# New prices in the clock that orders a hybrid decoder step: weight products, tile changes, scaled copies and a port shared by VectorE and GpSimd

## The chip, the cores and the metric

The kernel runs on one core of one Trainium2 chip. The metric is device time in microseconds (us); a verdict compares medians of several runs. A core has five engines that work at the same time, each through its own list of instructions in order: TensorE (PE, matmuls; PEld is its weight load), VectorE (DVE), ScalarE (ACT), GpSimd (POOL) and SyncE (SP, which issues most transfers). An instruction waits for semaphores of other engines, and everything behind it on its engine waits with it.

## The reference, cut to what matters

One step of a one-layer decoder for a prompt of 256 tokens and eight samples of eight tokens, 320 rows in all, with shared weights:

```python
h = rmsnorm(x, norm_g)
u = h @ w_in                            # 2048 x 23664: inputs of both mixers, gates
o_a = gdn(u) * silu(z_a)                # gated DeltaNet, 16 qk heads, 32 v heads, chunks of 64
o_b = nsa(u) * silu(z_b)                # compressed, selected and window attention over paged caches
y = x + (sigmoid(m_a) * (o_a @ w_branch_a) + sigmoid(m_b) * (o_b @ w_branch_b)) @ w_out
```

The DeltaNet recurrence goes over the chunks of the prompt, for each head:

```python
v_new = u_c - w_c @ s
o = qg_c @ s + attn_c @ v_new
s = s * gl_c + kdec_c.T @ v_new
```

where `u_c` and `w_c` are solutions of a triangular system per chunk. For the samples the state of each (`state_gdn`) is read, stepped by eight tokens and written. In the attention, each sample gathers 16 blocks of keys through a page table.

## The kernel before, in words

**Weight products.** The 320 rows stand on the free axis, the features on the partitions. Weights are read in pieces of up to 1 MB (`wraw`) and split in two parts of a format that TensorE reads faster: ScalarE writes `whi`, a rounded copy, and VectorE or GpSimd `wlo` = `wraw` − `whi`. The rows are split alike (`hhi`, `hlo`; for the branch products `oah`, `oal`). Three products, `hhi`·`whi`, `hlo`·`whi` and `hhi`·`wlo`, each 128x128 by 128x320, add up in `acc`; there are two such accumulators, and 11,952 such products in all. `wpool` holds three pieces, `wsplit` four parts of each kind.

**Stages.** While the weights go by, the other work runs between the products: the norm of the rows, the prompt's attention, the samples' attention over compressed, window and selected pages (two streams of samples with ten page buffers each), then sixteen blocks of the DeltaNet, each for one qk head and its two v heads, and at last the branch products and `w_out`. A DeltaNet block `j` has a convolution (`xp`, `cv`), norms (`sq`, `bank`), the preparation (`kk`, `kq`, `A`, `at`, `R`), the inverse of the triangular system by doubling (`Xd`, `Ac`, `T`, `TTd`, `X`: products of 32x32 tiles with a step of VectorE between them), the chunk steps of the prompt (`vnz` on VectorE, from it on TensorE `p` and `ps`, and the new state `st` on VectorE) and the steps of the samples (`sS`, `vS`, `pu`, `ats`).

**What sets the order.** The order is made while the program is built. Every part is a stream, a Python generator that says before each step which engine it needs and which tiles. `Run.go` takes at each point the stream whose step could start earliest, by a clock that counts along; its rank breaks ties. The product stream `p_mm` has the last rank, 9: a weight product goes out where nothing else could start as early. The streams that split weights (`p_hi`, `p_lo`) come early when the parts run low. `p_lo` gives a part to GpSimd for the first four and, during the DeltaNet, for every fourth; else to VectorE.

The clock (class `Clock`) holds a time for each engine, the end of the last write and read of each tile, and a delay between engines (`WAIT`). `Timed` wraps every engine: it prices an instruction by its kind and size, calls `Clock.op`, which moves the engine's time, and then records the instruction itself. So a price decides where later instructions stand, and nothing else; each engine then runs its list in that order, and the waits between engines follow from the tiles. All recorded instructions have the line of the call in this wrapper (L320 before, L331 after), transfers L292 and L299.

The function `page` issues the read of one cache page. The page's number must be in a register of SyncE; `page` loads the 16 numbers of a sample in one go (`ptab`) when they are not at hand, and drops the numbers of another selected sample of the same parity, or of any compressed one, when it does.

Of the kernel before, what the change touches and what calls it, by code (L numbers as in the profile page):

```python
# [64 lines left out]
class Pack:  # L65
    def __init__(self, rows=P):
        self.at, self.parts, self.n, self.rows = {}, [], 0, rows
# [95 lines left out]
def _n(ap):  # L163
    n = 1
    for x in ap.ap[1:]:
        n *= x[1]
    return n


class Clock:  # L170
# [6 lines left out]
    def __init__(self):  # L177
        self.t = dict.fromkeys(("pe", "act", "dve", "pool", "sp", "dge", "dma"), 0.0)
        self.parts, self.cut, self.psum = {}, {}, set()
        self.slot = {}  # L180
        self.w, self.r = {}, {}
        self.last = (0.0, "sp")
        self.set, self.lock, self.narrow, self.cold = None, False, False, True

    def key(self, ap):
        n = ap.tensor.name
        k = self.slot.get(n)
        if k is None:
            return None
        if k[0] == "dscr":  # L190
            k = k, ap.offset
        if n in self.cut:
            k = k, ap.offset % 512 >= self.cut[n]
        if n in self.parts:
            width, step = self.parts[n]
            row, col = divmod(ap.offset, width)
            k = k, col // P, row // step
        return k
# [43 lines left out]
            self.set = name  # L242
            self.t["act"] += 1300

    def op(self, eng, ns, outs, ins):
        outs, ins = self.keys(outs), self.keys(ins)
        self.t[eng] = e = self.start(eng, outs, ins) + ns
        self.mark(eng, e, outs, ins)

    def dma(self, eng, nbytes, out, in_):  # L250
# [13 lines left out]
def _isap(x):  # L264
    return isinstance(x, bass.AP)


class Timed:


    def __init__(self, eng, name, clock):
        self.__dict__.update(eng=eng, name=name, clock=clock)

    def __getattr__(self, op):
        f = getattr(self.eng, op)
        if op == "preload_act_table_set":
            def f_(name):
                self.clock.table("exp" if name == EXPSET else "sqrt")
                f(name)
            return f_  # L280
        if not callable(f) or op == "value_load":
            return f

        def g(*a, **k):
            aps = [x for x in a if _isap(x)] + [x for n, x in k.items() if _isap(x) and n not in ("out", "accum_out")]
            outs = [x for x in (k.get("out"), k.get("accum_out")) if _isap(x)]
            if "out" not in k:
                outs.insert(0, aps.pop(0))
            n = _n(outs[0])
            if op == "dma_start":  # L290
                self.clock.dma(self.name, 4 * n * outs[0].ap[0][1], outs[0], aps[0])
                return f(*a, **k)  # L292
            if self.name == "pe":
                if op == "transpose":
                    ns = 109
                else:
                    kk, m = a[1].ap[0][1], _n(a[1])
                    if a[1].dtype == F32R:
                        ns = max(n / 2.4, 107)  # L299
                    else:  # L300
                        ns = max(n * 1.67, 107) if m > 32 else max(n / 2.1 + 13, 34)
                narrow = op != "transpose" and _n(a[1]) <= 32
                if self.clock.narrow and not narrow:
                    ns += 80
                self.clock.narrow = narrow
                if self.clock.cold:
                    ns *= 2
            elif self.name == "dve":
                if op in ("tensor_reduce", "reciprocal"):
                    n = _n(a[1])  # L310
                ns = 65 + n * (6.4 if op == "reciprocal" else 1) / 0.96
                if op == "scalar_tensor_tensor" or (op == "tensor_scalar" and len(aps) > 1):
                    ns += 62
            elif self.name == "act":
                self.clock.table(SETS.get(a[2] if len(a) > 2 else k["func"], None))
                ns = (50 if aps[0].tensor.name in self.clock.psum else 93) + n / 1.2 + (170 if "accum_out" in k else 0)
            else:
                ns = 100 + n * (1.9 if op == "tensor_tensor" else 1)
            self.clock.op(self.name, ns, outs, aps)
            return f(*a, **k)  # L320
        return g

# [103 lines left out]
def step(ctx: ExitStack, tc: tile.TileContext, I, O):  # L426
# [854 lines left out]
    def scores(e, b, npg, dst, kS, finish):  # L1281
# [39 lines left out]
        V.scalar_tensor_tensor(dst[:, npg * P:npg * P + 64], ns[:, :64], SCALE, newB[:, 56 - 8 * b:120 - 8 * b], op0=OP.mult, op1=OP.add)  # L1321

    def weighted(e, b, npg, x, vS, op):
        prev = None
        for quad in list(range(0, npg + 1, 4)) + [None]:
# [1003 lines left out]
```

## Time and profile before

| what | value |
| --- | --- |
| median of 3 runs | 2679.83 us (2678.03 to 2683.69) |
| the profiled execution | 2674.97 us, of which the span is 2673.2 |
| TensorE busy | 2578.5 us (96%) |
| VectorE busy | 1714.6 us (64%) |
| ScalarE busy | 1360.4 us (51%) |
| GpSimd busy | 678.1 us (25%) |
| read and written | 543.84 MB, mean 203 GB/s |

The page of the profile counts matmuls as pipelined, so a busy time of TensorE may hold slack. The clock of TensorE that the chip granted had a mean of 0.993. A row of a group reads: line, engine, operation, output <- inputs, tile, count | busy us, mean ns of one | idle us just before them and what ended it.

### The profile page before, as it was taken

To read this page: it belongs to the slowest core of one execution; us is meant where nothing else is said; L and a number is where in the kernel's file an instruction comes from. 1 tells how busy PE (TensorE), PEld (TensorE's weight loads), DVE (VectorE), ACT (ScalarE), POOL (GpSimd) and SP (SyncE) were. 2 spreads that over 40 slices of the span, in tenths; PEclk is the share of its full clock that TensorE was granted. 3 is DMA by queue.
4 is the path that set the end of the run, shared out by engine and by line. 5 is a ranking of instruction groups with operands and counts; after the bars stand their busy time and mean duration, and the time that the engine had idled before them with its cause. 6 is when DMAs were issued, how large, how long until landed. Compare 5 with 4: busy or idle time off the path is not lost. (4 is left out here: it accounts for less than half of the span.)

```text
span 2673.2 us, 58873 instructions
## 1 busy us (share of the span) xinstructions
PE 2578.5 (96%) x22228; PEld 2327.9 (87%) x22228; DVE 1714.6 (64%) x3740; ACT 1360.4 (51%) x3098; POOL 678.1 (25%) x929
## 2 busy tenths in 40 slices
PE   7999999999999999999999899988999989999999
PEld 6898888888888888899889888888988889999999
DVE  5554446555555655445987888988888875355543
ACT  5453443343443333336667666666666655444443
POOL 2000011000000000012454454555445444211111
PEclk9999999999999999999999999999999989999999
DMA  6647676878768898865355445444455456656554
GB/s 205 229 156 257 231 241 228 279 248 282 269 222 308 287 333 283 284 211 175 118 157 175 132 153 176 141 139 136 153 153 166 155 160 214 207 177 192 179 192 132
DMA packets 548671, 543.84 MB, mean 203 GB/s; under 512 B 32482, under 2 KB 452499, under 8 KB 548003
## 3 DMA queue, kind: packets, MB, share of 16 engines
q1 hardware_dynamic: 534308, 493.67, 57.7%
q0 software_dynamic: 14080, 46.41, 4.9%
q8 instruction: 175, 2.87, 0.4%
q14 instruction: 108, 0.88, 0.1%
HBM read 470.31 MB, written 69.67 MB: 202 GB/s over the span
## 5 line engine op out<-in xcount | busy, mean ns | idle before, releaser
L320 PE MATMUL acc<-hhi,whi 128*128 128x320 f32 (+1 forms) x3472 | 1156.1, 333 | 0.8 <-ACT whi L320 0.8
L320 PE MATMUL acc<-hhi,wlo 128*128 128x320 f32 (+1 forms) x3472 | 1078.1, 311 | 2.0 <-DVE wlo L320 1.4
L320 PE MATMUL acc<-hlo,whi 128*128 128x320 f32 (+1 forms) x3472 | 1076.4, 310 | 1.3 <-DVE hlo L320 1.1
L320 ACT ACTIVATE whi<-wraw 128x512 fp32r<-128x512 f32 (+1 forms) x996 | 626.1, 630 | 861.3 <-PE acc L320 791.5
L320 DVE TENSOR_TENSOR wlo<-wraw,whi 128x512 fp32r<-128x512 f32 x838 | 605.0, 725 | 510.0 <-ACT whi L320 503.9
L320 PEld LDWEIGHTS acc<-hhi,whi 128*128 128x128 f32 (+1 forms) x3472 | 657.4, 189 | 80.4 <-issue 65.8
L320 PEld LDWEIGHTS acc<-hlo,whi 128*128 128x128 f32 (+1 forms) x3472 | 657.8, 189 | 8.7 <-issue 2.5
L320 PEld LDWEIGHTS acc<-hhi,wlo 128*128 128x128 f32 (+1 forms) x3472 | 655.6, 189 | 3.6 <-DVE wlo L320 2.6
L320 POOL TENSOR_TENSOR wlo<-wraw,whi 128x512 fp32r<-128x512 f32 (+1 forms) x158 | 208.0, 1317 | 417.9 <-ACT whi L320 391.3
L320 DVE SCALAR_TENSOR_TENSOR cv<-xp,cw,cv 128x344 f32<-128x344 f32 x192 | 141.5, 737 | 28.5 <-ACT cv L320 26.1
L292 POOL DMA_DIRECT2D d_mz<-raw x48 | 26.4, 550 | 519.9 <-ACT raw L320 487.1
L320 PE MATMUL acc<-oah,whi 128*128 128x320 f32 x512 | 158.2, 309 | 0.0
L320 PE MATMUL acc<-oal,whi 128*128 128x320 f32 x512 | 158.2, 309 | 0.0
L320 PE MATMUL acc<-oah,wlo 128*128 128x320 f32 x512 | 158.2, 309 | 0.0
L320 ACT ACTIVATE kT<-nt 128x512 f32<-128x512 f32 x80 | 47.7, 596 | 101.7 <-PE ns L320 55.9
L320 DVE COPY kT<-nt 128x512 f32<-128x512 f32 x80 | 55.2, 691 | 64.5 <-PE ns L320 41.5
L320 PEld LDWEIGHTS acc<-oah,whi 128*128 128x128 f32 x512 | 96.1, 188 | 0.0
L320 PEld LDWEIGHTS acc<-oal,whi 128*128 128x128 f32 x512 | 96.1, 188 | 0.0
L320 PEld LDWEIGHTS acc<-oah,wlo 128*128 128x128 f32 x512 | 96.1, 188 | 0.0
L320 POOL TENSOR_TENSOR vx<-v,pk_gdn 128x512 fp32r<-128x512 f32 x64 | 71.2, 1112 | 74.4 <-DVE v L320 56.1
L320 PE MATMUL pp<-cpg,Pk 128*32 128x512 f32 x608 | 83.0, 602 | 0.0
L320 PE MATMUL nt<-pk_const,spg 128*128 128x128 f32 x512 | 68.3, 274 | 0.5 <-DMA spg<-cache_k_sel 0.5
(420 smaller groups left out, 3629.5 us busy)
## 6 DMA issues: line engine op xcount, KB each, us to landing
wraw<-w_in SPq DMA_DIRECT2D x136, 1024.0 KB
wraw<-w_in SPq DMA_DIRECT2D x97, 512.0 KB
cpg<-cache_k_cmp SPq DMA_DIRECT2D x128, 256.0 KB
cpg<-cache_v_cmp SPq DMA_DIRECT2D x128, 256.0 KB
spg<-cache_k_sel SPq DMA_DIRECT2D x128, 256.0 KB
spg<-cache_v_sel SPq DMA_DIRECT2D x128, 256.0 KB
wraw<-w_branch_a SPq DMA_DIRECT2D x32, 1024.0 KB
sS<-state_gdn SPq DMA_DIRECT2D x32, 512.0 KB
```

The lines of the kernel that those rows point to most:

```text
L292: return f(*a, **k)
L320: return f(*a, **k)
```

## The change

Five prices of the clock change:

1. A product of the fast format (`F32R`): the time for n columns was n / 2.4 ns, at least 107; now (n + 32) / 2.4. For 320 columns 133 and 147 ns.
2. A product in full precision whose stationary tile has at most 32 columns (`m`): was n / 2.1 + 13 ns, at least 34; now n × 0.42, 0.105 or 0.47, at least 13, by the number of rows of that tile (`kk`) and by n.
3. A change of tile size: was 80 ns when TensorE leaves a tile with `m` up to 32; now 170 ns whenever it goes from a full tile to one with 64 or fewer rows or columns, or back.
4. ScalarE: 100 ns more where a copy has a second operand in memory (a scale or bias).
5. A shared port: an operation of VectorE with two inputs in SBUF and a two-input operation of GpSimd cannot overlap; the later one starts at the earlier one's end. The delay goes into the engine's time.

```diff
-    def op(self, eng, ns, outs, ins):
+    def op(self, eng, ns, outs, ins, port=False):
         outs, ins = self.keys(outs), self.keys(ins)
-        self.t[eng] = e = self.start(eng, outs, ins) + ns
+        s = self.start(eng, outs, ins)
+        if port:
+            a, b = self.port["pool" if eng == "dve" else "dve"]
+            if a <= s < b:
+                s = b
+            self.port[eng] = s, s + ns
+        self.t[eng] = e = s + ns
         self.mark(eng, e, outs, ins)
...
                     if a[1].dtype == F32R:
-                        ns = max(n / 2.4, 107)
+                        ns = max((n + 32) / 2.4, 107)
+                    elif m > 32:
+                        ns = max(n * 1.67, 107)
                     else:
-                        ns = max(n * 1.67, 107) if m > 32 else max(n / 2.1 + 13, 34)
-                narrow = op != "transpose" and _n(a[1]) <= 32
-                if self.clock.narrow and not narrow:
-                    ns += 80
-                self.clock.narrow = narrow
+                        ns = max(n * (0.42 if kk > 32 else 0.105 if n > 32 else 0.47), 13)
+                part = op != "transpose" and (kk <= 64 or m <= 64)
+                if self.clock.narrow != part:
+                    ns += 170
+                self.clock.narrow = part
...
+                port = op in ("tensor_tensor", "scalar_tensor_tensor") and sum(x.tensor.name not in self.clock.psum and _n(x) > 1 for x in aps) > 1
...
-                ns = (50 if aps[0].tensor.name in self.clock.psum else 93) + n / 1.2 + (170 if "accum_out" in k else 0)
+                ns = (50 if aps[0].tensor.name in self.clock.psum else 93) + n / 1.2 + (170 if "accum_out" in k else 100 if len(aps) > 1 else 0)
             else:
-                ns = 100 + n * (1.9 if op == "tensor_tensor" else 1)
-            self.clock.op(self.name, ns, outs, aps)
+                port = op == "tensor_tensor"
+                ns = 100 + n * (1.9 if port else 1)
+            self.clock.op(self.name, ns, outs, aps, self.name in ("dve", "pool") and port)
```

The instructions are the same, except for the loads of page numbers; the order differs. Three places follow.

TensorE around the 6576th weight product, in the DeltaNet stage. `p` and `ps` from `vnz` are the chunk steps of the prompt, `st`,`wq` the next one's first product, `kk` and `pu` belong to other blocks and to the samples' steps. Before, a chunk step there:

```order
L320 MATMUL bank<-pk_const,tl 108x128
L320 MATMUL p_20718<-vnz_14558,kde 128x128 x2
L320 MATMUL acc<-hhi,whi 128x320
L320 MATMUL acc<-hlo,whi 128x320
L320 MATMUL acc<-hhi,wlo 128x320
L320 MATMUL ps<-vnz_14558,at 128x128 x2
...
L320 MATMUL ps<-st,wq 128x128 x2
L320 MATMUL bank<-pk_const,hist 128x96
```

Three to six weight products stand between the steps of the recurrence. Now:

```order
L331 MATMUL ps<-R,pk_gdn 128x294
L331 MATMUL p_20981<-vnz_14461,kde 128x128 x2
L331 MATMUL ps<-vnz_14461,at 128x128 x2
L331 MATMUL ps<-st,wq 128x128 x2
L331 MATMUL kk<-kqP 128x128 x2
L331 MATMUL kk<-kqS 128x128
L331 MATMUL p_21012<-vnz_14460,kde 128x128 x2
L331 MATMUL pu<-vx,k_20212 128x512
L331 MATMUL ps<-vnz_14460,at 128x128 x2
L331 MATMUL ps<-st,wq 128x128 x2
...
L331 MATMUL p_21037<-vnz_14461,kde 128x128 x2
```

Three chunk steps follow one another with no weight product between them; the piece without products goes on behind them with an inverse.

VectorE between the last two chunk steps of the fourth DeltaNet block; `vnz` is what the next `p` and `ps` on TensorE wait for. Before:

```order
L320 TENSOR_TENSOR vnz_14557<-uP,ps 64x256
L320 SCALAR_TENSOR_TENSOR ats_14553<-row,gc,pk_gdn 128x4x16 x2
L320 TENSOR_TENSOR Xd<-A,pk_gdn 32x192 x2
L320 SCALAR_TENSOR_TENSOR st<-st,ends,p_19149 128x128 x2
L320 TENSOR_TENSOR at<-kq,at 128x512
L320 TENSOR_TENSOR wlo<-wraw,whi 128x512
L320 TENSOR_TENSOR sS<-sS,pu 128x512
L320 TENSOR_TENSOR ats_14553<-ksq,ats_14553 128x8x16
L320 TENSOR_TENSOR Xd<-A,pk_gdn 32x192 x2
L320 TENSOR_REDUCE Ac<-Xd 128x48
L320 TENSOR_TENSOR vnz_14558<-uP,ps 64x256
```

Now:

```order
L331 TENSOR_TENSOR vnz_14460<-uP,ps 64x256
L331 STREAM_TRANSPOSE v_19736<-hl 128x256
L331 SCALAR_TENSOR_TENSOR A<-row,gc,pk_gdn 128x128 x2
L331 TENSOR_TENSOR wlo<-wraw,whi 128x512
L331 SCALAR_TENSOR_TENSOR st<-st,ends,p_19799 128x128 x2
L331 TENSOR_TENSOR sS<-sS,pu 128x512
L331 SCALAR_TENSOR_TENSOR A<-row,gc,pk_gdn 128x4x16 x2
L331 SCALAR_TENSOR_TENSOR cv<-xp,cw,cv 128x344
L331 TENSOR_TENSOR vnz_14461<-uP,ps 64x256
```

Another mix of the same kinds of work stands between the two, and there is less of it.

SyncE's queue where the selected pages (`spg`) are read; `TENSOR_LOAD ptab` is a load of page numbers, the `ISA` rows set the address of the next transfer. Before:

```order
L292 DMA spg<-cache_v_sel 128x512
L1128 TENSOR_LOAD ptab
L292 ISA
L292 DMA spg<-cache_k_sel 128x512
...
L292 DMA wraw<-w_in 128x8x256
```

Now:

```order
L299 DMA spg<-cache_k_sel 128x512
L1139 TENSOR_LOAD ptab
L299 ISA
L299 DMA spg<-cache_k_sel 128x512
L1139 TENSOR_LOAD ptab
L299 ISA
L299 DMA spg<-cache_k_sel 128x512
```

The page numbers are loaded again after a single page: the pages of two samples of the same parity alternate, and each load drops the other's numbers. In the whole program there are 34 such loads in place of 16.

More of the change, by code (lines that the diff above doesn't have):

```diff
@@ L183, in __init__ @@
         self.set, self.lock, self.narrow, self.cold = None, False, False, True
+        self.port = {"dve": (0.0, 0.0), "pool": (0.0, 0.0)}
     def key(self, ap):
```

## The prediction, as it went on record

> **What bounds the kernel now.** I read the page's first part, then busy time by stretches of the program, then what TensorE waited for.
>
> ```profile
> span 2673.2 us, 58873 instructions
> PE 2578.5 (96%) x22228; PEld 2327.9 (87%) x22228; DVE 1714.6 (64%) x3740; ACT 1360.4 (51%) x3098; POOL 678.1 (25%) x929
> L320 PE MATMUL acc<-hhi,whi 128*128 128x320 f32 (+1 forms) x3472 | 1156.1, 333 | 0.8 <-ACT whi L320 0.8
> L320 PE MATMUL acc<-hhi,wlo 128*128 128x320 f32 (+1 forms) x3472 | 1078.1, 311 | 2.0 <-DVE wlo L320 1.4
> 0.00:100.00 100.00, 86.25 (x495) 72.85 (x496) 59.06 (x135) 54.15 (x95) 16.73 (x18) 1.00 0.68 211
> 820.00:1020.00 200.00, 198.22 (x2341) 163.74 (x2340) 113.93 (x218) 75.11 (x129) 6.51 (x12) 1.00 0.92 320
> 1300.00:2220.00 920.00, 850.57 (x8328) 791.87 (x8328) 791.80 (x1867) 590.69 (x1577) 469.48 (x656) 0.98 0.49 151
> 2300.00:2400.00 100.00, 100.00 (x684) 100.00 (x683) 44.30 (x60) 43.31 (x75) 21.03 (x19) 1.00 0.60 183
> ```
>
> TensorE is busy 2578.5 of 2673.2 us, and both kernels issue the same matmuls, so an order can win back little more than the 94.7 us of idle time. Where that sits is in the stretches (start:end, length, busy time of PE, weight load, VectorE, ScalarE and GpSimd with counts, granted clock, DMA share, GB/s). The last hundred-microsecond row has none: TensorE runs without a gap. The start has 13.75 us. The DeltaNet stage, 1300 to 2220 us, has 920 − 850.57 = 69.4 us, three quarters of all, with VectorE busy 791.80 of 920 (86%) and the clock at 0.98. So the stage is bound by TensorE nearly everywhere and by VectorE here and there; the rest of the program by TensorE alone. The selection stage, 820 to 1020, stands apart: 1.8 us idle, but DMA at 0.92.
>
> ```profile
> PE p L320 <- DVE vnz L320: 15.8, 13, 4.3
> PE ps L320 <- DVE vS L320: 11.8, 6, 2.9
> PE ps L320 <- DVE R L320: 11.0, 7, 2.4
> PE bank L320 <- DVE sql L320: 7.0, 7, 2.3
> PE ps L320 <- DVE TTd L320: 5.9, 10, 0.9
> ```
>
> These are TensorE's longest waits (total us, times, longest), all for VectorE. The timeline of one shows why it is late:
>
> ```profile
> 1501.41 0.31 PE L320 MATMUL acc<-hlo,whi 128*128 128x320 f32 x1
> 1501.55 0.31 PE L320 MATMUL acc<-hhi,wlo 128*128 128x320 f32 x1
> 1507.64 1.70 DVE L320 TENSOR_TENSOR Xd<-A,pk_gdn 32x192 f32<-32x192 f32 x2
> 1507.67 1.45 POOL L320 TENSOR_TENSOR wlo<-wraw,whi 128x512 fp32r<-128x512 f32 x1
> 1510.46 1.09 PE L320 MATMUL p<-vnz,kde 128*128 128x128 f32 x4 [2.37 <-DVE vnz L320]
> 1511.62 0.47 PE L320 MATMUL acc<-hlo,whi 128*128 128x320 f32 x1
> 1511.88 0.47 PE L320 MATMUL acc<-hhi,wlo 128*128 128x320 f32 x1
> ```
>
> TensorE's order has `p<-vnz` at a fixed place; VectorE has a queue ahead of `vnz`. Two `Xd` take 1.70 us while GpSimd's `wlo` of 1.45 us runs, and TensorE stands 2.37 us. Behind the gap weight products start 0.26 us apart instead of 0.14: half clock for a while.
>
> **The change, part by part.** It removes no operation. Five prices of the planner's clock move, and with them the order.
>
> *(a) VectorE's queue between chunk steps.* These rows are VectorE's groups in 1300 to 2220, and `Xd` in all its instances (least, median, longest ns):
>
> ```profile
> L320 DVE TENSOR_TENSOR wlo<-wraw,whi 128x512 fp32r<-128x512 f32 x228 | 183.2, 807 | 33.6 <-ACT whi L320 32.7 <-PE bank L320 0.2
> L320 DVE SCALAR_TENSOR_TENSOR cv<-xp,cw,cv 128x344 f32<-128x344 f32 x165 | 121.6, 737 | 18.7 <-ACT cv L320 16.7
> L320 DVE TENSOR_TENSOR Xd<-A,pk_gdn 32x192 f32<-32x192 f32 x60 | 42.6, 709 | 0.9
> L320 DVE TENSOR_TENSOR sS<-sS,pu 128x512 f32<-128x512 f32 x62 | 41.9, 677 | 5.5 <-PE pu L320 5.1
> L320 DVE SCALAR_TENSOR_TENSOR A<-row,gc,pk_gdn 128x128 f32<-128x128 f32 (+1 forms) x90 | 39.1, 486 | 1.6 <-DMA row<-d_gc 1.6
> L320 DVE SCALAR_TENSOR_TENSOR st<-st,ends,p 128x128 f32<-128x128 f32 x94 | 28.0, 338 | 2.1 <-PE p L320 1.7
> L320 DVE TENSOR_TENSOR ats<-ksq,ats 128x128 f32<-128x128 f32 x15 | 11.8, 784 | 0.0
> L320 DVE TENSOR_TENSOR at<-kq,at 128x512 f32<-128x512 f32 x15 | 10.3, 684 | 1.5 <-PE kq L320 1.4
> L320 DVE TENSOR_TENSOR Xd<-A,pk_gdn x64: 326/354/4124, 1279.0 to 2168.4; 32x192 f32<-32x192 f32 x64
> ```
>
> `Xd`'s mean is twice its median: a shared port would do that, and the old clock knew none. Priced by these means, the VectorE rows of the fourth block shown with the change hold, before, 4 × 0.709 + 0.807 + 0.677 + 2 × 0.338 + 0.784 + 0.684 = 6.5 us, 7.9 with the smaller ones, against 5.8 us of TensorE's own work between the same two steps; after, 4 × 0.486 + 0.807 + 2 × 0.338 + 0.677 + 0.737 = 4.8, 5.2 with the smaller ones, against 5.5. I did this sum for every pair of neighbouring chunk steps, with TensorE's side from the distances between starts in the trace. Before, VectorE has more to do than TensorE in 28 of 32 pairs, 29.5 us together. After, 22 of 33 pairs, 30.0 us; but 21.6 of these lie in the five pairs of (b), and the other 28 hold 8.4. So outside (b) the excess falls by 1 − 8.4/29.5 = 71%. The waits that come from a place in VectorE's queue are `vnz`, `R` and `sql`, 15.8 + 11.0 + 7.0 = 33.8 us; `vS` and `TTd` are steps of a chain, and stay. Gain 0.71 × 33.8 = **24 us**. Bounds: 33.8, and 0 if the next instruction in VectorE's queue is as late as the one before was; I stay near the upper one, since the sum fell in nearly all pairs.
>
> *(b) Pieces without weight products.* With the products now priced at 147 ns instead of 133, the filler runs dry: in five places TensorE's order holds small matmuls alone, 161 of them after the 6576th weight product (17.3 us by the distances of the trace), and 72, 50, 83 and 86 later (8.7, 1.6, 4.2, 3.0 us). Before, only two of 34 and 40 do. There each chain stands open:
>
> ```profile
> 2186.00:2214.00 28.00, 22.47 (x278) 19.15 (x277) 16.64 (x42) 14.76 (x40) 8.04 (x9) 0.82 0.48 158
> 2186.40 0.45 PE L320 MATMUL ps<-TTd,A 32*32 32x32 f32 x32
> 2187.97 0.45 PE L320 MATMUL ps<-T,X 32*32 32x32 f32 x32 [1.12 <-DVE X L320]
> 2192.17 0.65 PE L320 MATMUL ps<-TTd,A 32*32 32x32 f32 x32
> 2193.24 0.45 PE L320 MATMUL ps<-T,X 32*32 32x32 f32 x32 [0.41 <-DVE X L320]
> 2194.55 0.44 PE L320 MATMUL ps<-TTd,A 32*32 32x32 f32 x16 [0.86 <-DVE TTd L320]
> ```
>
> Here the last inverse runs with little cover: hops of 1.57, 1.07 and 1.31 us, mean 1.32, of which TensorE works 0.45, so each hop leaves 0.87 us open. By the sum of (a) the first piece has 30.3 us of VectorE work against 17.4 of TensorE's, 12.8 us too many, and the others 2.8, 2.5, 2.1 and 1.4: together 21.6. By hops, the order has six of an inverse (from `TTd` to `T` and back) in the first piece: 6 × 0.87 = 5.2 us, inside the same time. Price **+22 us**; bounds 10 (half of the queue can move behind the piece) and 44 (all at the half clock that the stretch above nears, 0.82).
>
> *(c) Clock.* The mean of 0.98 over 920 us costs up to 0.02 × 920 = 18 us. Long gaps get fewer with (a), new ones come with (b): **−5**, bounds −10 and +5.
> By the Trainium skill ("TensorE: Matmul & The Clock Gate", Part 1: The HAM clock gate) the clock halves only after a window of about 3.4 us without work; by that rule (c) is nothing and the pieces' short gaps stay at full clock, the sum 5 us higher. This trace speaks against it: 0.26 us spacing after a gap of 2.37 us, and 0.82 where no wait passes 1.12 us.
>
> *(d) SyncE and the selected pages.* The order holds 34 loads of page numbers where there were 16, since the two sample streams now alternate pages of samples that displace one another's numbers.
>
> ```profile
> 859.00 3.40 SPq L292 DMA_DIRECT2D spg<-cache_v_sel  x6
> 863.69 2.04 SPq L292 DMA_DIRECT2D spg<-cache_k_sel  x4
> ```
>
> Six page issues take 3.40 us, and 863.69 − 862.40 = 1.29 us pass before the next: one such load. 18 more hold SyncE's queue for 18 × 1.29 = 23 us; page transfers and the weight pieces are queued behind. Twenty page buffers cover some of it, and DMA at 0.92 is near its end already, with sample attention now done 468 products earlier. Without cover it costs 23; TensorE idled only 1.8 us in this stretch, so **+4**, an estimate from these two; bounds 0 and 23.
>
> *(e) Fewer switches.* Runs of weight products between other work fall from 845 to 778. The first product of a triple shows 333 ns against 311, 22 × 3472 / 845 = 90 ns for each run: 67 × 90 = 6 us, **−5**, bounds −6 and 0. The startup's other order of transposes and ten `wlo` more on GpSimd ahead of the stage: nothing, since VectorE is 57% busy there (113.93 of 200). ScalarE's 100 ns only moves starts: it is busy 64% of its stage.
>
> VectorE operations of one input are left out of the new port:
>
> ```profile
> L320 DVE TENSOR_SCALAR sm<-sm 128x4 f32<-128x4 f32 (+1 forms) x30 | 11.0, 365 | 0.5 <-ACT jk L320 0.5
> ```
>
> 365 ns for four elements is a wait for something. The Trainium skill ("GPSIMD Engine Reference", 8. Key points) has VectorE contend with GpSimd with two SBUF inputs and also "in a 2-port perf mode"; the new clock counts the first kind alone. By that rule these 30 still come late, 11 us at most, and (a) would be 24 less some of it.
>
> Sum: −24 + 22 − 5 + 4 − 5 = −8. The profiled execution took 2674.97 us (span 2673.2), the median of the three runs is 2679.83, 4.9 more; 2680 − 8 gives **2672 us**.
>
> **The rivals.**
>
> *Pieces hidden* (2650). VectorE's surplus in the pieces moves behind them, because what TensorE lacks there is small and the products are still to come: −24 − 5 + 4 − 5 = −30. For it: the same products follow, and at 2300 to 2400 TensorE has no gap while VectorE is 44% busy. Against it: the pieces' chains need each other's results, as in 2186 to 2214.
>
> *Pieces at double price* (2699), slower. One mechanism: in the piece after the 6576th product the chain runs uncovered, gap upon gap, and what TensorE does in it runs at half clock; 44 instead of 22, and the clock's gain is lost as (c) lies in the same gaps: −24 + 44 + 4 − 5 = +19. It decides once a piece costs over 1.4 times my price (30 us). For it: the clock of 0.82, and 28 − 22.47 = 5.5 us idle in 28. Against it: those 28 us had weight products among them, and cost no more.
>
> *The waits only move* (2679): VectorE's total is the same, at 86% of the stage; what waits less for `vnz` waits for `vS` or `TTd`. Then (a) is nothing, but (b) isn't an extra either, as its work is taken from elsewhere: 4 − 5 = −1. This is also what "the change doesn't do what it says" gives.
>
> **How the numbers follow.** A measurement of this kernel tells 0.2%, 5.4 us, from no change. Forecast 0.34 (2672; own range 2660 to 2680, so 0.22 faster, 0.12 same); pieces hidden 0.20, faster; double price 0.27, slower; waits move 0.19 (0.04 faster, 0.08 same, 0.07 slower, by (d) at its upper bound). Faster 0.46, same 0.20, slower 0.34. The range reaches somewhat beyond the hidden and the double case, for the bounds of (a) and (d): 2642 to 2702.
>
> **What would show it.** (a): waits for `vnz`, `R` and `sql` of some 10 us in all instead of 33.8. (b): five stretches without `acc`, the first of some 30 us, with TensorE idle 13 in it. (c): the stage's clock at 0.98 or more. (d): TensorE's idle time in the selection stage under 6 us. (e): the first product's mean near 331 ns. The forecast falls if the first piece takes over 40 us, if `spg` shows up among TensorE's waits with over 10 us, or if the stage's idle time stays at 69 with the pieces free.

## The result, and the profile after

The changed kernel is slower: 2710.67 us, median of 4 runs (2704.65 to 2714.42), against 2681.74 for the kernel before; the ratio is 1.011, with a 95% interval of 1.0092 to 1.0129. I had forecast 2672 in a range of 2642 to 2702. The profiled execution has a span of 2702.9 us.

The page's first part and two of its groups, and the stretches that answer to those shown of before (start:end, length, busy us of PE, weight load, VectorE, ScalarE and GpSimd with counts, granted clock, DMA share, GB/s):

```profile
span 2702.9 us, 58920 instructions
PE 2594.8 (96%) x22228; PEld 2339.9 (87%) x22228; DVE 1705.1 (63%) x3730; ACT 1356.9 (50%) x3098; POOL 689.5 (26%) x939
L331 PE MATMUL acc<-hhi,whi 128*128 128x320 f32 (+1 forms) x3472 | 1151.7, 332 | 1.8 <-ACT hhi L331 1.8
L331 PE MATMUL acc<-hhi,wlo 128*128 128x320 f32 (+1 forms) x3472 | 1078.7, 311 | 0.2 <-DVE wlo L331 0.2
0.00:100.00 100.00, 84.14 (x461) 66.26 (x462) 56.38 (x125) 49.80 (x87) 16.88 (x18) 1.00 0.72 223
800.00:1000.00 200.00, 197.25 (x2476) 162.66 (x2475) 114.28 (x220) 74.86 (x128) 6.16 (x11) 1.00 0.91 320
1300.00:2240.00 940.00, 861.42 (x8365) 800.84 (x8365) 788.75 (x1867) 589.43 (x1577) 464.64 (x657) 0.95 0.48 147
2330.00:2430.00 100.00, 100.00 (x684) 100.00 (x683) 44.40 (x60) 43.00 (x76) 20.42 (x18) 1.00 0.61 186
```

The loss is in the DeltaNet stage: 78.6 us idle there instead of 69.4, and the clock at 0.95 instead of 0.98. The start and the selection stage have 2.1 and 1.0 us more idle time, the end none. To say how much, I take the stage between the same two pieces of work, the starts of the 4981st and the 9051st weight product; in between both kernels issue the same 8887 matmuls. First before, then after:

```profile
1242.82:2237.12 994.30, 922.89 (x8887) 861.65 (x8885) 848.05 (x1988) 645.36 (x1709) 502.17 (x704) 0.98 0.49 151
```
```profile
1250.13:2266.23 1016.10, 935.68 (x8887) 873.14 (x8885) 844.42 (x1988) 643.93 (x1709) 498.64 (x704) 0.96 0.48 148
```

The stage takes 1016.1 − 994.3 = 21.8 us more. Of the rest of the spans' difference (2702.9 − 2673.2 = 29.7), 7.3 us lie ahead of it (1250.13 − 1242.82) and 0.6 behind. Of TensorE's waits after, these bear on the argument:

```profile
PE ps L331 <- DVE X L331: 12.8, 8, 4.5
PE ps L331 <- DVE TTd L331: 11.9, 12, 2.7
PE pu L331 <- POOL vx L331: 8.2, 5, 4.2
PE ps L331 <- DVE R L331: 7.2, 6, 2.5
PE ps L331 <- ACT oP L331: 5.8, 3, 5.0
PE ps L331 <- DVE vS L331: 4.1, 3, 2.3
PE bank L331 <- DVE sql L331: 3.0, 5, 1.0
PE p L331 <- DVE vnz L331: 2.9, 5, 1.3
```

`vnz`, `R` and `sql` fell from 33.8 to 13.1 us, as step (a) had it. `X`, `TTd`, `vx` and `oP` have grown in their place; 30 of their 38.7 us lie in the five pieces without weight products. The longest as a stretch, and some rows of TensorE's timeline in it:

```profile
1585.45:1628.44 42.99, 27.88 (x300) 20.94 (x299) 34.32 (x96) 22.22 (x71) 19.37 (x30) 0.74 0.36 112
```
```profile
1585.45 0.31 PE L331 MATMUL acc<-hhi,wlo 128*128 128x320 f32 x1
1588.94 0.51 PE L331 MATMUL bank<-sqh,meanr 128*128 128x320 f32 x1 [3.18 <-ACT xp L331]
...
1603.62 0.61 PE L331 MATMUL p<-vnz,kde 128*128 128x128 f32 x4
...
1618.11 1.35 PE L331 MATMUL ps<-pk_const,oP 128*128 128x128 f32 x4 [5.00 <-ACT oP L331]
...
1626.60 0.64 PE L331 MATMUL ps<-TTd,A 32*32 32x32 f32 x16 [0.85 <-DVE TTd L331]
...
1628.44 0.64 PE L331 MATMUL acc<-hhi,whi 128*128 128x320 f32 x1
```

From the 6576th weight product to the next one 43 us go by, for 17.3 us of TensorE's work. No engine is full in this piece: VectorE works 34.3 of 43, ScalarE 22.2, GpSimd 19.4. The rows show links over several engines, 5.00 us for ScalarE's `oP` the longest. In the next three VectorE is taken nearly all the time, 22.0 of 23.1, 5.6 of 6.3 and 14.3 of 14.9 us; in the fifth it works 4.5 of 10.5:

```profile
1846.43:1869.55 23.12, 13.32 (x135) 9.43 (x133) 21.96 (x65) 10.82 (x40) 13.05 (x16) 0.77 0.28 84
1925.66:1931.95 6.29, 2.42 (x102) 1.57 (x100) 5.61 (x18) 3.46 (x13) 2.67 (x5) 0.88 0.46 145
1985.08:1999.95 14.87, 6.87 (x161) 4.81 (x159) 14.31 (x35) 5.39 (x19) 7.54 (x12) 0.61 0.34 102
2217.24:2227.71 10.47, 5.81 (x173) 4.68 (x172) 4.48 (x15) 4.35 (x13) 3.61 (x4) 0.66 0.59 169
```

Some of VectorE's time there is spent on one slow operation. From the third of these four stretches:

```profile
1988.82 4.33 DVE L331 SCALAR_TENSOR_TENSOR cv<-xp,cw,cv 128x344 f32<-128x344 f32 x1
1989.91 1.04 POOL L331 TENSOR_TENSOR kb<-ktok,be 128x512 f32<-128x512 f32 x1
1990.91 1.03 POOL L331 TENSOR_TENSOR vx<-v,pk_gdn 128x512 fp32r<-128x512 f32 x1
...
1994.52 0.56 DVE L331 SCALAR_TENSOR_TENSOR cv<-xp,cw,cv 128x344 f32<-128x344 f32 x1
1994.74 0.65 PE L331 MATMUL ps<-T,X 32*32 32x32 f32 x32 [4.50 <-DVE X L331]
```

This `cv` takes 4.33 us, the next one 0.56, while GpSimd runs one operation behind another; TensorE waits 4.50 us for the `X` that stands behind it. A port that both share would do that, but no run separates it.

The five pieces take 43.0 + 23.1 + 14.9 + 10.5 + 6.3 = 97.8 us for the 34.8 us of work that I had counted, so 63 us are lost in them. VectorE is busy in 34.3 + 22.0 + 5.6 + 14.3 + 4.5 = 80.7 of them. Outside them TensorE's idle time in the stage fell from 71.4 to 38.9 us, and its busy time from 922.9 − 34.8 = 888.1 to 935.7 − 56.3 = 879.4. So the stage's account is 63.0 − 32.5 − 8.7 = 21.8 us.

Why the products stop in the first four can be read off while the order is made. The product stream asks at each tile whether it may start. A tile of z needs a free z buffer, of which there are three, and so the block three back must be done. Counting when that gate was first found shut and when it opened, in the planner's own clock, for the order after (before: never shut):

```
after product   shut for (planner's us)   between the two products on the chip (us)
6576            37.6                      43.0
7536            22.1                      23.1
7776             6.3                       6.3
8016            12.4                      14.9
```

So the planner foresaw these four pieces, to within 0 to 5 us. It takes whatever can start earliest, lets the products run ahead until the gate shuts, and has nothing left to fill with. The fifth piece, after the 8892nd product, is not the gate's. There the products are those of a branch, and their input is still being read:

```profile
2219.73 8.51 SPq L299 DMA_DIRECT2D ld<-d_ob  x8
2225.16 0.47 ACT L331 ACTIVATE hhi<-ld 128x320 fp32r<-128x320 f32 x1 [0.61 <-DMA ld<-d_ob]
```

### The profile page after: what moved, and what is told of

Same layout as the page of the kernel before. It is cut to its first block, busy times and chain, and to the rows that moved or that the text cites. A ratio compares the mean times of both kernels' runs of the same rounds, so it can differ in the third digit from the quotient of the medians.

```text
span 2702.9 us, 58920 instructions
## 1 busy us (share of the span) xinstructions
PE 2594.8 (96%) x22228; PEld 2339.9 (87%) x22228; DVE 1705.1 (63%) x3730; ACT 1356.9 (50%) x3098; POOL 689.5 (26%) x939
## 5 line engine op out<-in xcount | busy, mean ns | idle before, releaser
L331 DVE TENSOR_TENSOR wlo<-wraw,whi 128x512 fp32r<-128x512 f32 x828 | 596.7, 722 | 524.4 <-ACT whi L331 499.7
L331 POOL TENSOR_TENSOR wlo<-wraw,whi 128x512 fp32r<-128x512 f32 (+1 forms) x168 | 220.9, 1316 | 424.1 <-ACT whi L331 415.6
L331 DVE SCALAR_TENSOR_TENSOR cv<-xp,cw,cv 128x344 f32<-128x344 f32 x192 | 153.5, 800 | 18.4 <-ACT cv L331 14.7
```

## The experiments

All times of a run are given against runs of before on the same chip. "Stage" is always from the 4981st to the 9051st weight product; its loss is idle time of TensorE plus half of its busy time at half clock. This table has all of it; the runs are told one by one behind it. "Queue waits" are TensorE's waits for `vnz`, `R`, `sql` and `vS`; "pieces" is the sum of distances over 6 us between weight products; "pace" is VectorE's work over TensorE's in the planner's clock in the stage (605/815 = 0.742 before).

```
kernel                         ratio   95% interval     stage   idle  loss  queue waits  pieces  pace
before                         1                        994.3   71.4    89     45.6         0    0.742
the change                     1.0110  1.0092-1.0129   1016.1   80.4   115     17.2      97.8    0.694 + port
e1_no_port                     1.0104  1.0085-1.0122   1017.1   89.6   113     58.2       7.2    0.694
e2_only_port                   1.0185  1.0166-1.0205   1041.3  103.2   149     19.1     183.7    0.740 + port
e3_fill                        1.0096  1.0078-1.0113   1017.4   56.6    83     16.9     100.1    as the change
e4_hold600                     1.0275  1.0255-1.0295   1059.0  104.0   117     48.4       6.1    -
e5_only_product_price          1.0091  1.0073-1.0109   1017.2   86.7   108     59.9       6.1    0.696
e6_only_small_tiles            1.0267  1.0245-1.0288   1021.5   88.9   120     43.2      80.0    0.771
e7_no_port_vector_1p1          1.0043  1.0026-1.0060    993.8   71.1    85     35.4         0    0.761
e8_product_price_vector_1p1    1.0090  1.0073-1.0107   1000.4   76.3    95     38.3      18.6    0.763
e9_stage_only                  1.0090  1.0076-1.0104   1021.2   81.2   121     18.5      97.9    0.694 + port
e10_stage_vector_1p05          1.0064  1.0051-1.0077   1014.5   84.3   110     54.2      12.7    0.727
e14_stage_vector_1p08          1.0053  1.0036-1.0070   1005.4   72.2   101     53.7         0    0.747
e11_stage_vector_1p10          1.0010  1.0000-1.0019    996.8   71.5    87     35.3         0    0.761
e12_stage_vector_1p15          1.0029  1.0020-1.0039   1003.8   75.5   101     37.1      47.6    0.796
e13_tight_gate                 1.0302  1.0285-1.0319   1071.1  126.2   168     28.7     164.6    0.763
e15_stage_pool_1p1             0.9986  0.9975-0.9997    988.3   66.8    83     46.5         0    0.761
e16_stage_pool_1p2             1.0066  1.0048-1.0084   1009.4   77.4   112     61.8         0    0.760
```

**Is it the port?** e1 leaves the port's delay out of the change, e2 adds it alone to before.

```diff
-            if a <= s < b:
+            if False:
                 s = b
```

> The change without the port's delay (the other four prices stay). Theory A, the closed gate: the port's delay makes the planner see DeltaNet steps later, weight products fill up to the gate of z (three z tiles), and the pieces without products that follow cost 63 us over their own work. Then this order has no such piece over 5 us, TensorE at half clock is back near 38 us from 89, the stage's idle time under 60 us, and the time is 2665 to 2685. Theory B, VectorE sets the stage's time and the pieces only show it in one place: the same work waits elsewhere, time 2700 to 2715. In either case the waits for vnz, R and sql (13.1 us with the change, 33.8 before) tell whether the port's delay is what shortened them: back over 25 us if it is.

> Before with the port's delay alone. Theory A: by the planner's order there are five long pieces without products, 60 us of TensorE work by the distances of the trace against 35 with the whole change; so slower than the change, 2715 to 2740, half clock over 100 us. Theory B: what matters is the mix of all five prices; 2680 to 2700.

e2 came out as theory A had it: 2731 us, seven distances over 6 us, 184 us of pieces, with VectorE busy in 163 of them. (Its stage has 89 of the other matmuls fewer; they run behind it, where 9 us are added.) `TTd` and `oP` lead its waits, while `vnz` and `R` are short:

```profile
PE ps L329 <- DVE TTd L329: 21.9, 9, 5.5
PE ps L329 <- ACT oP L329: 14.6, 7, 4.9
...
PE p L329 <- DVE vnz L329: 4.4, 8, 0.8
PE ps L329 <- DVE R L329: 3.9, 5, 1.2
```

e1 did not: one piece, of 7.2 us, and 2707 us all the same, in the range of theory B. The loss has another form, above all one wait that the port's delay had removed:

```profile
PE ps L331 <- DVE R L331: 39.5, 15, 5.6
PE p L331 <- DVE vnz L331: 13.1, 13, 2.4
```

So the port's delay makes the long pieces, which lose 63 us, and it takes as much away elsewhere: TensorE's idle time outside them is 38.9 us with it and 89.6 in e1, of which `R` alone is 39.5 − 7.2 = 32, and its busy time there is 13 us less. In the time it nets nothing. The other four prices cost about as much by themselves.

**What is a piece bound by?** e3 keeps the change's order and puts weight products into the pieces whose sum is thrown away (they go to the accumulator that the next real product starts anew).

```diff
+                def gate():
+                    r = pj["acc"] < 2 and q["ready"](f)
+                    if not r and pj["gdn"] and pj["acc"] < 2 and len(pj["lo"]) > pj["mm"]:
+                        if not idle:
+                            idle.append(new())
+                        idle.append(1)
+                        if len(idle) % 2:
+                            T.eng.matmul(idle[0], pj["hi"][pj["mm"]][:, 0], q["hi"][:, 0], start=True, stop=True)
+                    return r
```

> The change with the same order, and some 225 weight products added in the pieces whose sum is thrown away (33 us of TensorE work at full clock), so that TensorE has something to do there. Nothing else moves. If half clock is a price of its own: half clock falls from 89 us to under 50, the time by 10 to 20 us to 2690 to 2700. If the pieces are bound by the chains over VectorE, ScalarE and GpSimd alone: the clock is up but the time stays within 5 us of the change, 2705 to 2716. If TensorE itself is short: slower by up to 33 us.

```profile
L574 PE MATMUL acc<-hhi,whi x222: 302/310/636, 1492.7 to 2007.5; 128*128 128x320 f32 x111
```
```profile
1255.30:2272.70 1017.40, 960.82 (x9109) 900.94 (x9108) 844.54 (x1988) 644.11 (x1709) 499.79 (x704) 0.97 0.48 148
```

2706.5 us: 222 products more, the stage's half clock down from 89 to 61 us, and the stage the same, 1017.4 against 1016.1. Of the 222, 190 lie in four of the pieces, none in the one after the 8892nd product. The five take 42.5, 24.3, 16.3, 9.8 and 7.2 us against 43.0, 23.1, 14.9, 10.5 and 6.3 unfilled. So TensorE's idle time there is free, and no gain from its clock shows: the other engines set the length, VectorE above all, busy in 82.6 of the 100.1 us. That the fillers cost what the clock gained is not excluded, since three of the four filled pieces grew by 0.9 to 1.4 us. No run makes VectorE's work in a piece shorter, so its part is read from the traces and not tested.

**Holding the products back.** e4 takes a weight product only if nothing else could start within 600 ns.

```diff
-                s = s, x[3]() if callable(x[3]) else x[3]
+                s = s + (600 if x[3] == 9 and self.hold() else 0), x[3]() if callable(x[3]) else x[3]
```

> All five prices, but during the DeltaNet the planner takes a weight product only if nothing else could start within 600 ns after it; its order has no closed gate and no piece without products. Theory A: the gain of the shorter waits is kept and the pieces are gone: 2645 to 2675, faster than before. Theory B: 2700 or more. A third way: the held products leave TensorE idle in small gaps instead, 40 us and more over the stage, and the time is near before's, 2675 to 2690.

```profile
PE p L331 <- DVE vnz L331: 35.4, 31, 1.8
PE ps L331 <- DVE TTd L331: 15.6, 46, 1.2
```

2754 us, in theory B's range of 2700 or more. The form is that of the third way, though its time was too low: the long pieces are gone, and many short waits stand in their place, 31 for `vnz` and 46 for `TTd`, 1.1 and 0.3 us in the mean. TensorE's idle time in the stage grows by 33 us. Its work there, with time at half clock counted half, grows by 37 more, from 905 to 942; why is open.

**Single prices.** e5 has only the first, e6 only that of small tiles.

```diff
-                        ns = max(n / 2.4, 107)
+                        ns = max((n + 32) / 2.4, 107)
```

> Before with the first price alone, (n + 32) / 2.4 for weight products. Its order has no closed gate. Theory C, the pace: what counts is how dear TensorE's work is in the clock against VectorE's. In the clock of before both are too cheap in the stage (TensorE 815 us planned against 905 worked, VectorE 605 against 792 in 920 us); with TensorE alone made dearer the order puts TensorE's steps where VectorE isn't ready in truth. Then waits for R, vnz and sql rise from 33.8 us to over 45, and the time is 2695 to 2715, near the change without the port (2707). Theory D, no rule: any other order loses, because ranks and buffers were chosen for the order of before; then the waits that rise aren't these, with a time anywhere from 2680 to 2720.

> Before with the price of small tiles alone: TensorE's other work gets cheaper (785 us planned in the stage instead of 815), VectorE's is the same. The planner's gate of z closes five times, 50 us in its own clock. Theory C: waits for R, vnz and sql stay under 34 us, and the loss is in the pieces: half clock over 50 us, time 2690 to 2710. Theory D: the same time with no relation to the gate.

e5 is as theory C had it, with 30.0 + 16.9 + 2.2 = 49.1 us of waits for `R`, `vnz` and `sql`, against 33.8, and 2700 us:

```profile
PE ps L329 <- DVE R L329: 30.0, 12, 5.0
PE p L329 <- DVE vnz L329: 16.9, 20, 3.1
```

e6 has the pieces (80 us) and 27 us more in the stage, but 37.1 us of waits for `R`, `vnz` and `sql` where theory C had under 34, and its 2750 us were not expected by either: the stage starts 46 us later. The trace shows 39.8 us without a weight product after the 4752nd, at the end of the samples' attention, until new weights arrive:

```profile
1242.60 1.15 ACT L331 ACTIVATE whi<-wraw 128x512 fp32r<-128x512 f32 x2 [12.51 <-DMA wraw<-w_in]
```

That is the products running dry at another place, with VectorE busy in 11.9 of the 39.8 us. A tile change's price alone was not tried.

**The pace.** e7 takes e1 and prices VectorE 10% higher, e8 does the same with e5.

```diff
+                ns *= 1.1
             elif self.name == "act":
```

> The change without the port's delay, but with each operation of VectorE priced 10% higher, so that both engines are dearer than before by about the same share. No closed gate in its order. Theory C: the waits for R, vnz and sql fall from 55 us (change without the port) to 15 to 30, no piece appears, and the time is 2655 to 2685. Theory D: 2695 to 2720, like the other orders.

> The product price alone and VectorE 10% dearer. One closing of the gate, 10.6 us in the planner's clock. Theory C: as the run before, plus a piece that costs about 10 us: 2660 to 2695. Theory D: 2695 to 2720.

e7 against e1 is the clearest pair: the same prices but for VectorE's share, 23 us less in the stage, and `R` back from 39.5 to 9.6:

```profile
PE ps L332 <- DVE vS L332: 13.6, 8, 3.3
PE p L332 <- DVE vnz L332: 11.2, 11, 2.5
PE ps L332 <- DVE R L332: 9.6, 8, 3.1
```

In time it reached 2687, two more than expected; its trace has the stage 12.6 us later than that of before. e8 missed theory C and fell into theory D's range: the stage is 1000.4 us instead of e5's 1017.2, but it starts 15 us later than in before, and the time is 2701.

**The stage alone.** e9 to e12 and e14 keep the old prices up to the DeltaNet stage, so that the order is that of before up to the 4581st product. e9 has the whole change from there; e10, e14, e11 and e12 have it without the port and with VectorE 5, 8, 10 and 15% dearer.

```diff
-    pj["gdn"] = True
+    pj["gdn"] = clock.late = True
...
+                if self.clock.late:
+                    ns *= 1.1
             elif self.name == "act":
```

> The change's five prices from the start of the DeltaNet stage on, the old prices ahead of it: the order up to the 4581st weight product is that of before, and the stage has the same closings of the gate as the change. If some 7 us of the change's loss come from its order ahead of the stage, as the two profiles have it, then 2698 to 2706, 1.0065 to 1.0095 of before. If that was chance between profiles: 2707 to 2714.

> Old prices ahead of the stage; in it the change without the port's delay and VectorE 5% dearer. No closed gate. Theory C: between the run without the port (R, vnz and sql 53 us) and the one with 10% (22 us): 30 to 40 us of these waits, stage near 1005 us, 2685 to 2697.

> As the run with 10%, VectorE 8% dearer. No closed gate. Theory C: between 5% (2698) and 10% (2684): 2682 to 2692. Under 2676 would be a version faster than before.

> As the run before, VectorE 10% dearer. No closed gate. Theory C: stage 990 to 998 us as in the run with 10% throughout, and the loss ahead of it is gone: 2672 to 2684, no difference from before that can be told. Over 2690 would say that the pace theory explains the waits but not the time.

> As the run before, VectorE 15% dearer. The gate of z closes once, 32.6 us in the planner's clock. Theory C: waits for R, vnz and sql under 22 us, but one piece of 30 to 45 us with 15 to 25 us of it lost to idle time and half clock: 2685 to 2700.

e9 is 2707.7, ratio 1.0090 against the change's 1.0110, with overlapping intervals. Its time lies in the range for chance, its ratio in the other one, so it does not decide whether some 5 us or none belong to the order ahead of the stage. The traces' 7.3 us can't be held to: with one and the same order there, the stage starts at 1242.8 us in the trace of before and at 1245.6 to 1252.4 in the eight of e9 to e16, and 1250.1, the change's, lies among them. Already the 501st product starts at 123.6 us in the traces of before and of e10, and at 125.6 to 128.6 in the seven others. With VectorE 5, 8, 10 and 15% dearer the time goes 2698, 2694, 2684 and, with one piece of 39.4 us, 2689. The first two cannot be told apart, the last two only just. That is theory C with its turning point: too cheap, and TensorE waits for VectorE; too dear, and the products run into the gate. By its numbers it missed in part: e10 and e14 are 1 and 2 us over what was expected, e10's stage is 1014.5 us where some 1005 were, e10's wait is for `vS` (26.6 us) more than for `R`, `vnz` and `sql` (27.6), and e12 has 27.6 us of these where under 22 were expected.

**The gate alone.** e13 is e11 with the gate opening one block later.

```diff
-        okz = lambda f, j=j: pos["g2"] >= j - 2 and pos["g3"] >= j - 2
+        okz = lambda f, j=j: pos["g2"] >= j - 1 and pos["g3"] >= j - 1
```

> As the run with VectorE 10% dearer in the stage (2684 us, no closed gate), with one thing changed: the gate of z opens one block later, so that it closes twelve times, some 135 us in the planner's clock. All prices are equal, so the pace is the same. If a closed gate costs time by itself (theory A's second half): TensorE's idle time and half clock rise, 2710 to 2745. If the pieces only collect waits that would come anyway: 2680 to 2695.

```profile
1252.40:2323.50 1071.10, 944.94 (x8887) 877.92 (x8885) 825.24 (x1988) 647.05 (x1709) 501.65 (x705) 0.94 0.46 141
```

Equal prices, a gate that shuts a dozen times, and 76 us more (2760.5), beyond what was expected: the stage grows by 74. So a shut gate costs time by itself. Eleven pieces take 164.6 us, and VectorE is busy in 151.4 of them: while the products are shut out, TensorE can only follow VectorE. The opposite, a fourth z buffer, was not tried on the chip.

**GpSimd too.** e15 and e16 take e11 and price GpSimd 10 and 20% higher in the stage.

```diff
                 ns = 100 + n * (1.9 if port else 1)
+                if self.clock.late:
+                    ns *= 1.1
```

> VectorE and GpSimd both 10% dearer in the stage (GpSimd 407 us planned instead of 370; it works 465 in 920 us). No closed gate. Theory C carried to GpSimd: TensorE's waits for vx (7.2 us with VectorE alone) and for vS fall; 2668 to 2684.

> VectorE 10% and GpSimd 20% dearer in the stage (443 us planned). No closed gate. Theory C: waits for vx under 4 us; 2665 to 2684.

Both lose the wait for `vx`, as expected, 7.2 us to 0.4 and none. The wait for `vS` should have fallen too; from e11's 13.6 us it rose in both. First e15, then e16:

```profile
PE ps L340 <- DVE vS L340: 18.4, 9, 3.0
PE ps L340 <- DVE R L340: 12.0, 11, 2.1
PE p L340 <- DVE vnz L340: 9.9, 11, 2.3
...
PE pu L340 <- POOL vx L340: 0.4, 1, 0.4
```
```profile
PE ps L340 <- DVE vS L340: 31.1, 11, 3.0
PE p L340 <- DVE vnz L340: 21.0, 16, 4.0
```

e15 is the fastest of all, 2675.6 us (10 runs, 2670.88 to 2680.42), 0.14% under before, with an interval that just leaves out no change; as the best of sixteen it is nothing to build on. e16 missed and loses 0.7%, with TensorE waiting for `vS` and `vnz`. That VectorE, beside a dear GpSimd, is too cheap again would explain it, but is not shown.

## Why the prediction was wrong

**(a) VectorE's queue, −24: right.** `vnz`, `R` and `sql` fell by 33.8 − 13.1 = 20.7 us. I had left out `vS` as a link of a chain; it fell too, from 11.8 to 4.1. All of TensorE's idle time outside the pieces fell by 71.4 − 38.9 = 32.5 us. e1 and e2 show that the port's delay did it: without it `R` alone waits 39.5, and with it alone the three come to 4.4 + 3.9 + 3.6 = 11.9.

**(b) Pieces without products, +22: this step failed.** The places and TensorE's work in them were read rightly from the order (34.8 us, five pieces), but they cost 63 us, beyond my upper bound of 44, and the first took 43.0 us, over the 40 that I had named as a sign of being wrong. Pricing a piece by VectorE was right for the greater part; the size was wrong, in two terms.

- VectorE's work beyond TensorE's in the pieces was 80.7 − 34.8 = 45.9 us, not 21.6. In the first piece it was 34.3 instead of 30.3. In the others I had 2.8, 2.5, 2.1 and 1.4 us too many, and measured are 13.3, 4.0, 10.1 and 1.5. My sum went by pairs of chunk steps. The pair that holds the second piece runs from 1854.1 to 1902.5 us and has 141 weight products behind the piece; in such a pair they count as cover for VectorE's work, and on the chip they came after it.
- In the remaining 17.1 us VectorE stands idle as well, 8.7 of them in the first piece and 6.0 in the fifth: links through several engines, or, in the fifth, transfers. I had taken them to lie inside VectorE's time. The 0.87 us per hop that I had measured at the end of the stage counted one kind of link, the inverse; the longest wait in the first piece was another, 5.0 us for `oP`.

With 63 in place of 22 my sum gives −24 + 63 − 5 + 4 − 5 = +33. Measured are 29, of which the traces place 21.8 in the stage; where the other 7 belong is open (e9).

**(c) Clock, −5: wrong way, but no term at all.** Half clock in the stage grew from 37.5 to 88.7 us, of which 53.2 lie in the pieces and 35.5 outside. In e3 the stage had 27 us less of it and won nothing. By the Trainium skill ("TensorE: Matmul & The Clock Gate", Part 1: The HAM clock gate) the clock is set by windows of 3413 ns; the stretches at half clock in this stage, before and after, are 3.413, 6.827, 10.240 and 17.067 us, whole numbers of such windows, so that much of the page agrees. That a window must be idle altogether doesn't: in the 3.413 us ahead of the half clock at the prediction's gap of 2.37 us TensorE had worked 1.05 us.

**(d) SyncE's page numbers, +4: not seen.** Idle time in the selection stage is 200 − 197.25 = 2.75 us, against 1.8.

**(e) Fewer switches, −5: about right.** TensorE's work at full clock in the stage fell from 905 to 901 us; the first product's mean from 333 to 332.

**The rivals.** "Pieces at double price" (2699) had the side right, and its point of decision, a piece over 30 us. Of its mechanism the first half holds, a chain that runs uncovered, gap upon gap; the second, half clock, was there (0.74 in the first piece), but e3 speaks against it as the price. "The waits only move" is what the port's delay comes to by e1, through two effects of some 63 us that cancel, not through nothing. I had given the slower side 0.34.

**What lies behind both losses** is balance, as far as the runs go. In the stage the clock of before had TensorE 10% too cheap (815 us planned, 905 worked) and VectorE some 29% (605 planned, 848 in the row of before), but their pace was one that works. The change brings TensorE near the truth (872 planned, 901 worked) and adds the port to VectorE. The one without the other puts TensorE's steps ahead of VectorE (e1, e5); the port without the other, or on top, lets products run into the gate (e2, e9). A run-ahead that is bounded by three z buffers turns a planned delay into a stop. Shown are the first direction by e1 to e7 and e10 to e11, the second by e11 to e12 with 5 us, and the cost of a shut gate by e13. Not shown is a rule that ranks all orders, and theory D, that ranks and buffers suit the order of before, is not ruled out: e8 came out in its range, e14 has a pace between e10 and e11 and 65 us at half clock where they have 58 and 31, and e16, at the pace of e15, is 20 us slower. The spread among orders of about equal pace is larger than the 8 us that I had forecast.

## What to carry to other kernels

A truer clock doesn't make a better order: a planner that takes the earliest start follows the ratio of its engines' prices, and one price made true by itself shifts waits from one engine's queue to another's or to a buffer's end. Before believing a new order, look for the stretches where the filler is missing, and ask which bounded buffer or late transfer shut it off. Price such a stretch by itself: first the work of the fullest engine between its two ends, without the fillers behind it as cover, then the time in which that engine waits too. Here these were 80.7 and 17.1 of 97.8 us. And where the planner keeps a clock, print when its streams found their gates shut: here it had the 43 us of the first piece as 37.6 before anything ran.

## What the runs showed of the hardware

TensorE idle in a piece that hangs on other engines is free to fill: 222 matmuls of 310 ns, half clock down by 27 us, and no change in time. Traces of the same order lie 5 us apart already at the 501st weight product (123.6 to 128.6 us), so a difference of that size at the start of one trace is not a finding. The half clock comes in whole windows of 3.413 us, also after a wait of 2.37 us. And a VectorE operation of 0.56 us took 4.33 while GpSimd worked without a break.
